# Turning rows of x and half results by VectorE blocks and a DRAM bounce instead of TensorE transposes, at the end of a decoder step

## The chip, the cores and the metric

The kernel runs on one core of one Trainium2 chip, in one launch. The metric is device time in microseconds (us) of that core, the median of several runs; lower is better. In the rows below PE is TensorE (PEld its weight loads), DVE is VectorE, ACT is ScalarE, POOL is GpSimd, and SP, SyncE, issues most of the DMAs. DMAs can also be issued from the ACT and POOL queues.

## The reference

One inference step of one decoder layer over 512 prompt rows and 8 x 4 sample rows, d_model 1024, all in float32. The part that the change touches is the end of the layer:

```python
    x = x + _rmsnorm(m, norm_mix_post[l])
    f, ffn_state = _conv_ffn(_rmsnorm(x, norm_ffn_pre[l]), ffn_prev, w_up[l], ffn_conv_w[l], ffn_conv_b[l], w_down[l])
    x = x + _rmsnorm(f, norm_ffn_post[l])

def _conv_ffn(h, prev, w_up, conv_w, conv_b, w_down):
    u = h @ w_up
    u, conv_state = _causal_dwconv(u, prev, conv_w, conv_b)
    val, gate = jnp.split(u, 2, axis=-1)
    return (jax.nn.gelu(gate, approximate=True) * val) @ w_down, conv_state
```

So each of the 544 token rows of `f` (1024 wide, summed over 4096 inner columns) is divided by its root mean square, multiplied by a gain, and added to `x`; the outputs are `y_p` (512 x 1024) and `y_s` (32 x 1024), token by token.

## The kernel before

Every float32 matrix is split into a high and a low part (`wh`/`wl`, `fH`/`fL`), and a product is three matmuls (high x high, high x low, low x high). Most of the kernel works transposed: feature on the partition, token on the free axis. The down projection's result is held in eight tiles `ft0` to `ft7`, tile c being features 128c to 128c+127 by 544 tokens. `HALF` cuts the tokens into half a=0 (tokens 0 to 255) and half a=1 (tokens 256 to 543: two prompt tiles and the 32 sample rows). The 4096 inner columns are eight groups q of four 128-blocks (`CH` = 4); `down(q, c, a, done)` adds group q to tile c, half a: 12 matmuls into a PSUM bank (`pmdn`), and then one VectorE addition into `ft` (`down_done`, or `last_done` for the last group).

The end of the kernel does the two halves differently.

- Half a=1 is finished transposed. For the last group (`QL`), a loop over c runs `down(QL, c, 1, last_done(c, acc))`. `last_done` adds the bank into `ft`, ScalarE squares the tile, and VectorE adds the square into `acc`; the square of tile 7 goes to `sq7`. `finish_b` then sums `acc` and `sq7` over the partitions with TensorE (`pst`), makes the reciprocal root (ScalarE and VectorE), scales the eight `ft` tiles on VectorE and adds x (`x1r`, read back from DRAM, feature by token) on GpSimd. `rows_t(2)`, `rows_t(3)`, `rows_t(4)` turn these tiles into token rows with TensorE transposes (`pyo`), ScalarE copies them to `yo`, and a DMA writes them.
- Half a=0 is finished token by token. Its last group is computed straight into token rows: `tokens(i, kk)` makes a 128 token x 512 feature bank (`ptok`) for token tile i and feature half kk, for (0,0), (0,1) and (1,0). The bank of (1,1) is cut in two banks of 256 features, `ends(0)` and `ends(1)` (`pend`), the last matmuls that a norm needs. The sum over the seven earlier groups sits in `ft` and is turned into token rows by TensorE: `turned(i, kk)` makes four transposes into `pfo`, and ScalarE copies them to `frow`; for (1,1) two float32 matmuls by the identity inside `ends` add it into the bank. `tokens_done` adds the bank to `frow` on VectorE, squares on ScalarE, multiplies by the gain `gpost` on GpSimd; `rstd`/`tokens_out` give the root and the output row, with x in token rows: `xtok[0, kk]`, turned by TensorE in `x1_rows` and copied by ScalarE, and for i=1 read from the PSUM bank `px`.

The order of the work: TensorE, ScalarE and VectorE run the end in the order in which the code records it. A `slot()` first runs what was left for this turn (`result(...)`, in front, and `later(k, f, ...)`, behind), so what `later` holds stands behind the additions of the bank that just ended. Three banks of group QL-1 (c = 5, 6, 7 of half a=0, the list `held`) are kept back and run after the loop, to cover the root of half a=1. SP's order is set by the scheduler in the loop and is written order after it.

Of the kernel before, what the change touches and what calls it, by code (L numbers as in the profile page):

```python
# [11 lines left out]
F32 = mybir.dt.float32  # L12
# [5 lines left out]
P = 128  # L18
# [49 lines left out]
DNS = 5  # L68
LAST_PLACES = {29: ('p3', 'p1', 'a22'), 30: ('p3', 'p1', 'a22'), 31: ('p1', 'a22')}
# [52 lines left out]
def hawk_step(ctx, tc, I, O):  # L122
# [1599 lines left out]
    def x1_rows(i, kk):  # L1722
        px = PX(f"px1{i}_{kk}")
        for j in range(4):
            pe.transpose(px[:, j * P:(j + 1) * P], x1r[4 * kk + j][:, i * P:(i + 1) * P], ident)
        return px

    def x1_again():
        for c in range(8):
            x1r[c] = S(f"x1r{c}")  # L1730
            nc.sync.dma_start(out=x1r[c][:, 0:NT], in_=x1d[c])
        yield 3
        for kk in range(2):
            px = x1_rows(0, kk)
            xtok[0, kk] = S(f"xtok0_{kk}")
            act.copy(xtok[0, kk][:, 0:512], px)
            yield 0.5
# [61 lines left out]
    def finish_b(acc):  # L1799
# [6 lines left out]
        for c in range(8):  # L1806
# [3 lines left out]
            if c % 2:  # L1810
                yield 0.5

    def rows_t(i, between=None):
# [3 lines left out]
        for kk in range(2):  # L1817
# [4 lines left out]
            if between and not kk:  # L1822
                between()
# [17 lines left out]
    def turned(i, kk):  # L1841
        px = PX(f"pfo{i}_{kk}")
        for j in range(4):
            pe.transpose(px[:, j * P:(j + 1) * P], ft[4 * kk + j][:, i * P:(i + 1) * P], ident)
        if i not in frow:
            frow[i] = RAW(f"frow{i}")
        later(1, act.copy, frow[i][:, kk * 512:(kk + 1) * 512], px)
# [15 lines left out]
    def tokens_done(i, kk, ps):  # L1863

        fr = frow[i][:, kk * 512:(kk + 1) * 512]
        add(fr, fr, ps)
# [3 lines left out]
        g = gpost[:, kk * 512:(kk + 1) * 512]  # L1870
# [11 lines left out]

    def ends(z):
        ps = PM(f"pend{z}")
        o = ps[:, 0:256]
        for k in range(CH):
# [3 lines left out]
            pe.matmul(o, fh, wh, start=k == 0, stop=False, skip_group_check=True)  # L1890
            if k == 0:
                for j in range(2):
                    pe.matmul(ps[:, j * P:(j + 1) * P], ft[4 + 2 * z + j][:, P:2 * P], ident, start=False, stop=False,
                              skip_group_check=True)
# [7 lines left out]
    def ends_gain(z, o):  # L1902
        mul(fgs[1, 1][:, 256 * z:256 * z + 256], o, gpost[:, 512 + 256 * z:768 + 256 * z])

    def tokens_out(i, r, z):
        x_ = xtok[i, z][:, 0:512]
        o = x_ if i == 0 else fgs[i, z]
# [90 lines left out]
```

## Time and profile before

| what | value |
|---|---|
| median of 3 runs | 974.34 us (974.23 to 974.61) |
| the profiled execution: its own time | 973.95 us |
| its span, first to last instruction | 972.2 us |
| TensorE clock granted over the span | 0.999 |
| busy share: PE, DVE, ACT, POOL | 99%, 78%, 57%, 17% |
| instructions: PE matmuls, DVE, ACT, POOL | 7634, 1599, 1349, 282 |

The profiled execution is 1.75 us longer than its span, and 0.39 us below the median. The span is what rows of the trace tell of; times in the rows are us from its start, and the end of the kernel is at 972.2 us. A row of the timeline gives the start, the duration (of all x instructions together), the engine, the line, the operation, the tiles written and read, and in brackets how long the engine stood idle before it and what ended that.

### The profile page before, as it was taken

The numbers are of one execution on the slowest core, as the hardware profiler recorded it, in microseconds if no ns is written. First come the engines' busy times: TensorE is split into PE (matmuls) and PEld (weight loads), VectorE is DVE, ScalarE is ACT, GpSimd is POOL, SyncE is SP. The second block draws the span as 40 slices with busy tenths as digits, with TensorE's granted clock in tenths as the row PEclk, the third lists the DMA queues.
The fourth block names the chain that finished last, engine by engine and source line by source line (L and its number), as shares of the span: only waits on it lengthen the run. The fifth ranks groups of instructions, "written<-read, shape, count | busy, mean of one in ns | idle before, by whom it ended". The sixth has DMA issues, their size and how long they took to land.

```text
span 972.2 us, 20023 instructions
## 1 busy us (share of the span) xinstructions
PE 963.0 (99%) x7634; PEld 955.2 (98%) x7634; DVE 756.3 (78%) x1599; ACT 553.9 (57%) x1349; POOL 167.9 (17%) x282
## 2 busy tenths in 40 slices
PE   9999999999999999999999999999999999999997
PEld 8999999999999999999999999999999999999996
DVE  5777888857858555599967888787888888888875
ACT  6544443467476425566767665655555555656653
POOL 2242000003406330230010111111011101020024
PEclk9999999999999999999999999999999999999999
DMA  7775535532334547135157575857576766668612
GB/s 229 236 213 180 151 89 147 162 93 87 108 110 128 179 115 189 52 121 186 45 117 182 128 198 123 192 130 181 136 181 157 171 155 156 170 145 219 201 31 92
DMA packets 234203, 143.07 MB, mean 147 GB/s; under 512 B 25012, under 2 KB 218940, under 8 KB 234076
## 3 DMA queue, kind: packets, MB, share of 16 engines
q1 hardware_dynamic: 224300, 120.21, 41.8%
q0 software_dynamic: 9696, 19.42, 11.8%
q10 hardware_dynamic: 112, 2.17, 0.6%
q8 instruction: 60, 0.98, 0.4%
q14 instruction: 35, 0.29, 0.1%
HBM read 115.59 MB, written 15.17 MB: 134 GB/s over the span
## 4 chain that ended last, share of the span: by engine, by line
PE 94%; DVE 3%; ACT 1%; issue 0%; DMA 0%; POOL 0%; SPq 0%; DVEq 0%; ACTq 0%; POOLq 0%
PE pmin L163 20%; PE pmdn L163 19%; PE pux L1527 16%; PE puy L1527 8%; PE pq L1527 6%; PE pmlo L163 5%; PE pmao L163 5%; PE pmout L163 4%; PE puz L1527 4%; PE pg L163 1%; PE pvp L163 1%; PE psc L163 1%; PE ptok L163 1%; DVE wl_e L166 0%; DMA pt<-pd 0%
## 5 line engine op out<-in xcount | busy, mean ns | idle before, releaser
L163 PE MATMUL pmin<-hH,wh_in 128*128 128x256 f32 (+1 forms) x568 | 164.0, 291 | 0.0
L163 PE MATMUL pmin<-hL,wh_in 128*128 128x256 f32 (+1 forms) x568 | 162.4, 288 | 0.0
L163 PE MATMUL pmin<-hH,wl_in 128*128 128x256 f32 (+1 forms) x568 | 159.1, 288 | 0.0
L163 PE MATMUL pmdn<-fH,wh_dn 128*128 128x256 f32 (+1 forms) x448 | 129.2, 288 | 0.0
L163 PE MATMUL pmdn<-fH,wl_dn 128*128 128x256 f32 (+1 forms) x448 | 129.0, 288 | 0.0
L163 PE MATMUL pmdn<-fL,wh_dn 128*128 128x256 f32 (+1 forms) x448 | 128.9, 288 | 0.0
L163 PEld LDWEIGHTS pmin<-hH,wh_in 128*128 128x128 f32 x568 | 107.2, 189 | 1.2 <-issue 1.0
L163 PEld LDWEIGHTS pmin<-hL,wh_in 128*128 128x128 f32 x568 | 107.2, 189 | 0.1
L163 PEld LDWEIGHTS pmin<-hH,wl_in 128*128 128x128 f32 x568 | 104.7, 188 | 0.2 <-issue 0.2
L175 DVE SCALAR_TENSOR_TENSOR uc<-u,fv,uc 128x560 f32<-128x560 f32 x128 | 102.0, 797 | 1.7 <-ACT uc L1558 1.1
L163 PEld LDWEIGHTS pmdn<-fH,wl_dn 128*128 128x128 f32 x448 | 84.4, 188 | 0.0
L163 PEld LDWEIGHTS pmdn<-fL,wh_dn 128*128 128x128 f32 x448 | 84.3, 188 | 0.1
L163 PEld LDWEIGHTS pmdn<-fH,wh_dn 128*128 128x128 f32 x448 | 84.2, 188 | 0.1
L1655 ACT COPY u<-pux 128x272 f32<-128x272 f32 x52 | 20.1, 387 | 86.0 <-PE pux L1527 86.0
L166 DVE TENSOR_TENSOR u<-puy,u 128x240 f32<-128x240 f32 (+2 forms) x78 | 24.6, 344 | 49.6 <-PE puy L1527 32.5
L172 DVE TENSOR_TENSOR ft<-ft,pmdn 128x256 f32<-128x256 f32 (+1 forms) x104 | 45.1, 434 | 16.7 <-PE pmdn L163 16.7
L281 ACT ACTIVATE wh_in<-raw_in 128x512 fp32r<-128x512 f32 x70 | 42.2, 625 | 19.0 <-issue 10.6
L288 DVE TENSOR_TENSOR wl_in<-raw_in,wh_in 128x512 fp32r<-128x512 f32 x70 | 47.8, 693 | 1.0 <-ACT wh_in L281 1.0
L1558 ACT ACTIVATE uc<-u,fv 128x560 f32<-128x560 f32 x64 | 48.2, 755 | 0.0
L779 ACT ACTIVATE s<-s,st 128x256 f32<-128x256 f32 (+1 forms) x32 | 15.2, 475 | 53.0 <-DVE st L776 42.5
L166 DVE TENSOR_TENSOR wl_dn<-raw_dn,wh_dn 128x512 fp32r<-128x512 f32 x56 | 38.3, 685 | 3.6 <-ACT wh_dn L1476 3.6
L1465 POOL DMA_DIRECT2D raw_up_s<-raw_up_s x26 | 22.4, 861 | 93.2 <-DMA raw_up_s<-raw_up__11237 5.5
(743 smaller groups left out, 3374.9 us busy)
## 6 DMA issues: line engine op xcount, KB each, us to landing
raw_in<-in_w_in_dram SPq DMA_DIRECT2D x35, 512.0 KB
raw_dn<-in_w_down_dram SPq DMA_DIRECT2D x56, 256.0 KB
raw_up_s<-in_w_up_dram SPq DMA_DIRECT2D x25, 512.0 KB
raw_up_s<-raw_up_s POOLq DMA_DIRECT2D x26, 256.0 KB, 4.3
raw_ao<-in_w_attn_o_dram SPq DMA_DIRECT2D x8, 512.0 KB
raw_lo<-in_w_lru_o_dram SPq DMA_DIRECT2D x8, 512.0 KB
raw_out<-in_w_out_dram SPq DMA_DIRECT2D x8, 512.0 KB
pd<-pb SPq DMA_DIRECT2D x12, 256.0 KB
```

What stands on the lines that cost most here:

```text
L163: pe.matmul(out, l, r, start=start, stop=stop)
L166: dve.tensor_tensor(out=out, in0=a, in1=b, op=ALU.subtract)
L172: dve.tensor_tensor(out=out, in0=a, in1=b, op=ALU.add)
L175: dve.scalar_tensor_tensor(out=out, in0=a, scalar=s_, in1=b, op0=op0, op1=op1)
L281: act.activation(hl[0], raw, AF.Copy)
L288: (eng or dve).tensor_tensor(out=hl[1], in0=raw, in1=f32(hl[0]), op=ALU.subtract)
L779: act.activation(s3[:, j, :], s3[:, j, :], AF.Exp, bias=ng[:, j:j + 1], accum_out=sm[:, j:j + 1])
L1465: pool.dma_start(out=w["p4"], in_=w["p2"], accum_op=ALU.add)
L1527: pe.matmul(ps[:, :HN], w, x, start=start and k == 0 and i == 0, stop=stop and k == 3 and i == 2, skip_group_check=True)
L1558: act.activation(yt[j][:, 0:FLATU], u[:, 0:FLATU], AF.Copy, scale=fv[:, j:j + 1])
L1655: act.copy(e[nm_], z)
```

## The change

It takes 40 matmuls out of TensorE's program: every `turned`, `x1_rows` and `rows_t(2)` transpose, and the identity matmuls of `ends`. In their place `blocks` turns 32 x 32 blocks on VectorE (`dve.transpose`), both token tiles of half a=0 in one instruction per 128-feature tile, or the third tile alone. `rows_of` writes the block-turned buffer to DRAM with one DMA and reads it back with four, each of which gathers one block row, so that the row tile holds tokens on its partitions; inside a partition the features stay in blocks of 32, which `by_block` undoes in the access pattern of the reader. Six such bounces stand in the program: `f0` (the half results of features 0 to 511, tokens 0 to 255), `x0` and `x1` (the same for x), `f1` (half results of features 512 to 1023, two of its reads from ACT's queue), and `y0`, `y1` (the finished third output tile). ScalarE puts the x rows in order (`x_natural`); GpSimd copies the third output tile in order (`yo2`). The banks of `ends` are begun by a ScalarE copy of the half results into PSUM (`ends_begin`), so that the matmuls go on from it. SP's DMAs keep written order from the start of the last loop. `gpost` becomes two half tiles.

```diff
+TURNS = {0: (("f", 0), ("f", 1)), 1: (("f", 2), ("f", 3)), 2: (("x", 0), ("x", 1)), 3: (("x", 2), ("x", 3)),
+         4: (("x", 4), ("x", 5)), 5: (("x", 6),), 6: (("x", 7),)}
...
-    def x1_rows(i, kk):
-        px = PX(f"px1{i}_{kk}")
-        for j in range(4):
-            pe.transpose(px[:, j * P:(j + 1) * P], x1r[4 * kk + j][:, i * P:(i + 1) * P], ident)
-        return px
...
+    def blocks(buf, j, src, n):
+        o = buf[:, 0:512 * n].rearrange("p (b i c d) -> p c i b d", i=n, b=4, c=4)[:, j]
+        dve.transpose(o, src.rearrange("p (i b q) -> p i b q", i=n, b=4))
+
+    def rows_of(buf, n, rows, nm, queues=(nc.sync,)):
+        w = 512 * n
+        dr = drp.tile([P, w], F32, name=f"{nm}_blocks")
+        nc.sync.dma_start(out=dr, in_=buf[:, 0:w])
+        src = dr.rearrange("(a q) (b x) -> b q a x", a=4, b=4)
+        for b in range(4):
+            queues[b % len(queues)].dma_start(out=rows[32 * b:32 * b + 32, 0:w].rearrange("q (a x) -> q a x", a=4),
+                                              in_=src[b])
+        r = rows[:, 0:w].rearrange("p (a i c d) -> p i c a d", a=4, i=n, c=4)
+        return [r[:, i] for i in range(n)]
+
+    def by_block(ap):
+        return ap.rearrange("p (c a d) -> p c a d", a=4, d=32)
...
             if c % 2:
                 yield 0.5
+                for z in (c - 3, c - 2) + ((6, 7) if c == 7 else ()):
+                    if z >= 0:
+                        y2_block(z)
...
+    def y2_block(c):
+        if c % 4 == 0:
+            ybuf[c // 4] = T(f"yb{c // 4}")
+        blocks(ybuf[c // 4], c % 4, ft[c][:, 2 * P:3 * P], 1)
+        if c % 4 == 3:
+            yrow[c // 4], = rows_of(ybuf[c // 4], 1, S(f"yrow{c // 4}"), f"y{c // 4}")
...
-    def turned(i, kk):
-        px = PX(f"pfo{i}_{kk}")
-        for j in range(4):
-            pe.transpose(px[:, j * P:(j + 1) * P], ft[4 * kk + j][:, i * P:(i + 1) * P], ident)
-        if i not in frow:
-            frow[i] = RAW(f"frow{i}")
-        later(1, act.copy, frow[i][:, kk * 512:(kk + 1) * 512], px)
...
-        fr = frow[i][:, kk * 512:(kk + 1) * 512]
-        add(fr, fr, ps)
+        fr = T(f"fr{i}_{kk}")[:, 0:512]
+        add(by_block(fr), frow[i, kk], by_block(ps[:, 0:512]))
...
+    def ends_begin(z):
+        pends[z] = PX(f"pend{z}")
+        act.copy(by_block(pends[z][:, 0:256]), frow[1, 1][:, 2 * z:2 * z + 2])
...
-            pe.matmul(o, fh, wh, start=k == 0, stop=False, skip_group_check=True)
-            if k == 0:
-                for j in range(2):
-                    pe.matmul(ps[:, j * P:(j + 1) * P], ft[4 + 2 * z + j][:, P:2 * P], ident, start=False, stop=False,
-                              skip_group_check=True)
+            pe.matmul(o, fh, wh, start=False, stop=False, skip_group_check=True)
...
+    def x_natural(i, z):
+        xnat[i, z] = S(f"xnat{i}_{z}")[:, 0:512]
+        act.copy(by_block(xnat[i, z]), xtok[i, z])
...
     def tokens_out(i, r, z):
-        x_ = xtok[i, z][:, 0:512]
-        o = x_ if i == 0 else fgs[i, z]
-        stt(o, fgs[i, z], r, x_, ALU.mult, ALU.add)
+        o = fgs[i, z]
+        stt(o, o, r, xnat[i, z], ALU.mult, ALU.add)
...
+    order_.enter_context(tc.manual_schedule(engines={nc.sync.engine}))
     for c in range(8):
         down(QL, c, 1, last_done(c, acc))
...
-        if c in (3, 5):
-            turned(c // 5, 0)
...
+        for what, z in TURNS.get(c, ()):
+            if what == "f":
+                later(1, block2, "f", ft, frow, z)
+                if z == 3:
+                    later(1, rows2, "f", frow, 0)
+            else:
+                later(1, block2, "x", x1r, xtok, z)
+                if z % 4 == 3:
+                    later(1, rows2, "x", xtok, z // 4)
...
     for _, q, c, a in held:
         down(q, c, a, down_done(q, c))
+        for z in range(4, 8) if c == HELD else ():
+            if z < HELD:
+                later(1, block2, "f", ft, frow, z)
+        later(1, block2, "f", ft, frow, c)
+        if c == 7:
+            later(1, rows2, "f", frow, 1, (nc.sync, act))
+            for i in range(2):
+                later(2, x_natural, i, 0)
         slot(0)
     for i, kk in ((0, 0), (0, 1), (1, 0)):
         ps = tokens(i, kk)
         if (i, kk) == (0, 0):
             slot(0)
-            turned(0, 1)
         slot(0)
+        if (i, kk) == (0, 1):
+            for z in range(2):
+                ends_begin(z)
         tokens_done(i, kk, ps)
+        if i == kk == 0:
+            for z in range(2):
+                x_natural(z, 1)
...
-    yo = [rows_t(2)]
+    yo2 = RAW("yo2")
+    for z in range(2):
+        pool.tensor_copy(by_block(yo2[:, 512 * z:512 * z + 512]), yrow[z])
+    yo = [lambda: nc.sync.dma_start(out=yp[2 * P:3 * P, :], in_=yo2)]
```

Three places of the program show how the order moves. The first is VectorE in the last loop: `ft`c is tile c of half a=1 taking its bank `pmdn_7_c_1`, and `acc31` takes the square that ScalarE made of it. Before:

```order
L172 TENSOR_TENSOR ft1_7004<-ft1_7004,pmdn_7_1_1_13223 128x288
L172 TENSOR_TENSOR acc31_13198<-acc31_13198,sq_ft1_1_13261 128x288
L172 TENSOR_TENSOR ft2_7154<-ft2_7154,pmdn_7_2_1_13247 128x288
L172 TENSOR_TENSOR acc31_13198<-acc31_13198,sq_ft1_2_13286 128x288
L172 TENSOR_TENSOR ft3_7258<-ft3_7258,pmdn_7_3_1_13266 128x288
L172 TENSOR_TENSOR acc31_13198<-acc31_13198,sq_ft1_3_13305 128x288
L172 TENSOR_TENSOR ft4_7386<-ft4_7386,pmdn_7_4_1_13291 128x288
```

After, with `fb0` the block buffer of the half results and `xb0` that of x:

```order
L174 TENSOR_TENSOR ft1_7004<-ft1_7004,pmdn_7_1_1_13218 128x288
L174 TENSOR_TENSOR acc31_13198<-acc31_13198,sq_ft1_1_13252 128x288
L1733 STREAM_TRANSPOSE fb0_13233<-ft2_7154 128x2x4x32
L1733 STREAM_TRANSPOSE fb0_13233<-ft3_7258 128x2x4x32
L174 TENSOR_TENSOR ft2_7154<-ft2_7154,pmdn_7_2_1_13238 128x288
L174 TENSOR_TENSOR acc31_13198<-acc31_13198,sq_ft1_2_13280 128x288
L1733 STREAM_TRANSPOSE xb0_13283<-x1r0_13057 128x2x4x32
L1733 STREAM_TRANSPOSE xb0_13283<-x1r1_13059 128x2x4x32
L174 TENSOR_TENSOR ft3_7258<-ft3_7258,pmdn_7_3_1_13266 128x288
L174 TENSOR_TENSOR acc31_13198<-acc31_13198,sq_ft1_3_13302 128x288
L1733 STREAM_TRANSPOSE xb0_13283<-x1r2_13061 128x2x4x32
L1733 STREAM_TRANSPOSE xb0_13283<-x1r3_13063 128x2x4x32
L174 TENSOR_TENSOR ft4_7386<-ft4_7386,pmdn_7_4_1_13288 128x288
```

Two block transposes now stand behind each addition of a square and ahead of the next addition of a bank.

The second is ScalarE behind the reciprocal root of half a=1 (`ry_o1`, `rw_o1`). Before, `pfo` was copied out between the squares `jk`:

```order
L1167 ACTIVATE ry_o1_13404<-pst_o1_13387,epst_95 128x288
L1168 ACTIVATE rw_o1_13405<-ry_o1_13404 128x288
L1868 ACTIVATE jk0_0_13460,ssq_13196<-frow0_13284 128x512
L1586 COPY frow0_13284<-pfo0_1_13450 128x512
L1868 ACTIVATE jk0_1_13479,ssq_13196<-frow0_13284 128x512
L418 ACTIVATE nst_t0_13484<-ssq_13196,epst_95 128x1
L1868 ACTIVATE jk1_0_13504,ssq_13196<-frow1_13330 128x512
```

After:

```order
L1169 ACTIVATE ry_o1_13419<-pst_o1_13399,epst_95 128x288
L1170 ACTIVATE rw_o1_13420<-ry_o1_13419 128x288
L1742 DMA frow1_13463<-f1_blocks_13464 32x4x256 x2
L1933 COPY xnat0_0_13477<-xrow0_13307 128x512
L1933 COPY xnat1_0_13479<-xrow0_13307 128x512
L1891 ACTIVATE jk0_0_13496,ssq_13196<-fr0_0_13494 128x512
L1933 COPY xnat0_1_13500<-xrow1_13377 128x512
L1933 COPY xnat1_1_13502<-xrow1_13377 128x512
L1910 COPY pend0_13529<-frow1_13463 128x256
L1910 COPY pend1_13531<-frow1_13463 128x256
L1891 ACTIVATE jk0_1_13535,ssq_13196<-fr0_1_13533 128x512
```

ScalarE now issues two of the reads of `f1`, which wait for the write to DRAM, and ahead of the square of `fr0_1` it has four row copies and the two copies that begin the banks `pend0` and `pend1` from `frow1`.

The third is SP's queue at the very end. Before:

```order
L1922 DMA gpost_13370<-in_norm_ffn_post_dram 128x1024
L1909 DMA out_0_dram<-xtok0_0_13219 128x512
L1909 DMA out_0_dram<-xtok0_1_13243 128x512
L1824 DMA out_0_dram<-yo2_13516 128x1024
L1824 DMA out_0_dram<-yo3_13569 128x1024
L1909 DMA out_0_dram<-fg1_0_13506 128x512
L1909 DMA out_0_dram<-fg1_1_13514 128x512
```

After, from the write of `f1` on:

```order
L1739 DMA f1_blocks_13464<-fb1_13416 128x1024
L1742 DMA frow1_13463<-f1_blocks_13464 32x4x256 x2
L1739 DMA y0_blocks_13484<-yb0_13470 128x512
L1742 DMA yrow0_13483<-y0_blocks_13484 32x4x128 x4
L1739 DMA y1_blocks_13523<-yb1_13517 128x512
L1742 DMA yrow1_13522<-y1_blocks_13523 32x4x128 x4
L1938 DMA out_0_dram<-fg0_0_13498 128x512
L1938 DMA out_0_dram<-fg0_1_13537 128x512
L1999 DMA out_0_dram<-yo2_13571 128x1024
L1845 DMA out_0_dram<-yo3_13608 128x1024
L1938 DMA out_0_dram<-fg1_0_13563 128x512
L1938 DMA out_0_dram<-fg1_1_13569 128x512
```

The outputs of token tile 0 (`fg0_0`, `fg0_1`) and all that follow now stand behind the writes and reads of `y0` and `y1`, each read behind its own write, and the last two outputs behind that of `yo2`.

38 lines of the change are left out of this document (21 added, 17 removed).

## The prediction

> **What bounds the kernel now.** I read the page first: the span, the busy shares and the chain that ended last.
>
> ```profile
> span 972.2 us, 20023 instructions
> PE 963.0 (99%) x7634; PEld 955.2 (98%) x7634; DVE 756.3 (78%) x1599; ACT 553.9 (57%) x1349; POOL 167.9 (17%) x282
> ...
> PE 94%; DVE 3%; ACT 1%; issue 0%; DMA 0%; POOL 0%; SPq 0%; DVEq 0%; ACTq 0%; POOLq 0%
> ```
>
> TensorE is busy for 99% of the span and carries 94% of the chain, so in most of the kernel a microsecond taken from its program is a microsecond gained. The change touches only the last 40 us, so the next view is the chain of waits there (start, duration, what).
>
> ```profile
> 932.20 0.44 PE px L1725 x4
> ...
> 937.86 0.44 PE pfo L1844 x4
> ...
> 946.51 0.97 PE pst_o L163 x4
> ...
> 953.09 0.44 PE pfo L1844 x4
> 953.52 5.58 PE ptok L163 x24
> 959.11 0.87 PE pyo L1820 x8
> ...
> 960.10 0.44 PE pend L1893 x4
> ...
> 963.58 0.12 PE pend L1896
> ```
>
> Up to 963.70 (963.58 + 0.12) the chain is one TensorE instruction behind the other, with no wait between them; the transposes are links of it. The other engines are hidden there, but only just, which the timelines of VectorE, ScalarE and TensorE show (in brackets the idle time before a row and who ended it).
>
> ```profile
> 933.23 0.44 DVE L1744 STREAM_TRANSPOSE ffn_rows_s<-sfT 128x256 f32<-128x256 f32 x1
> 933.59 0.42 DVE L172 TENSOR_TENSOR ft<-ft,pmdn 128x288 f32<-128x288 f32 x1
> ...
> 935.73 0.78 DVE L172 TENSOR_TENSOR ft<-ft,pmdn 128x288 f32<-128x288 f32 x2
> 937.48 0.46 DVE L172 TENSOR_TENSOR acc<-acc,sq_ft 128x288 f32<-128x288 f32 x1 [0.96 <-ACT sq_ft L1181]
> ...
> 938.82 0.46 DVE L172 TENSOR_TENSOR acc<-acc,sq_ft 128x288 f32<-128x288 f32 x1 [0.51 <-ACT sq_ft L1181]
> ...
> 942.46 0.46 DVE L172 TENSOR_TENSOR acc<-acc,sq_ft 128x288 f32<-128x288 f32 x1 [1.49 <-ACT sq_ft L1181]
> ...
> 945.50 0.45 DVE L172 TENSOR_TENSOR ft<-ft,pmdn 128x288 f32<-128x288 f32 x1
> ...
> 951.56 0.41 DVE L172 TENSOR_TENSOR ft<-ft,pmdn 128x256 f32<-128x256 f32 x1
> ```
>
> ```profile
> 940.02 0.57 ACT L1586 COPY frow<-pfo 128x512 f32<-128x512 f32 x1
> 940.60 1.28 ACT L1917 ACT_TABLE_LOAD   x1
> ...
> 945.98 0.45 ACT L1178 ACTIVATE sq<-ft 128x288 f32<-128x288 f32 x1 [0.89 <-DVE ft L172]
> ```
>
> ```profile
> 946.35 0.65 PE L163 MATMUL pst_o<-acc,ones 128*128 128x288 f32 x2
> 946.83 0.65 PE L163 MATMUL pst_o<-sq,ones 128*128 128x288 f32 x2
> ```
>
> VectorE adds the last bank of the last loop (945.50) only a moment before ScalarE squares it (945.98 to 946.43), and TensorE sums that square from 946.83 on. The slack between the square and its reader is 0.4 us. That is the narrowest place of the region, and the change puts VectorE work in front of it.
>
> **What goes from TensorE.** Ahead of the last bank stood two groups of `px` (four transposes each), three of `pfo`, and two of `pend` on line 1893, 0.44 us each, and the eight of `pyo` at 0.87: 7 x 0.44 + 0.87 = 3.95 us. Of that 4 x 0.44 = 1.76 stand ahead of the sum `pst_o`. The eight `px` behind the last bank and what follows them are not on the way to the last output row. If nothing else moved, the end would come 3.95 earlier, at about 970.4.
>
> **What comes to VectorE in the last loop.** Twelve block transposes of 256 columns stand between the addition of bank 0 and that of bank 7 (four of the half results, eight of x). The row of `ffn_rows_s` is the same operation on 128x256: 0.44 us, the next instruction 0.36 behind its start. Twelve make 12 x 0.36 = 4.3 us. Could they lie in the idle time of the additions to `acc` (0.51 each)? No: that idle time stands between the addition of a bank and the addition of its square, while the transposes stand behind the latter, ahead of the next bank. They lengthen the chain. What they do hide is ScalarE's extra delay: two waits were longer than 0.51, by 0.45 (937.48) and 0.98 (942.46), put there by the copies of `xtok` and `frow` and the table load in front of the squares. The copies go, and the table load now fits beside two transposes. So bank 7 is added at 945.50 + 4.3 - 1.4 = 948.4, its square is ready 0.93 later (945.50 to 946.43 before), at 949.3, and the second `pst_o` matmul begins there instead of at 946.83: 2.5 us late. TensorE would have been at the sum at 946.35 - 1.76 = 944.6 and idles some 4 us. The 1.76 is lost and 2.5 more is added to all that stands behind the root of half a=1.
>
> Both ends of the transposes' price: the row is the same operation at the same size, so I allow a seventh each way, 0.31 to 0.42, which is 0.6 to 0.7 us on the loop; what differs is that the new tile is written in runs of 32 elements. I take 0.36.
>
> **The second bounce of half results.** The bank that ends the first half's `ft7` was added at 951.56. Now it comes 2.5 later, and behind one block transpose more: 954.4. Then its own transpose, 0.8 with the addition ahead of it, and the buffer can leave at 955.0. The way through DRAM has a forerunner in this kernel, the attention's `pb` to `pd` to `pt` (write of 256 KB, then four reads), and its rows bound it.
>
> ```profile
> 114.17 0.34 SPq L824 DMA_DIRECT2D pd<-pb  x1
> 116.28 1.74 SPq L829 DMA_DIRECT2D pt<-pd  x4
> ...
> 143.57 0.34 SPq L824 DMA_DIRECT2D pd<-pb  x1
> ```
>
> ```profile
> 147.27 4.37 DMA pt<-pd
> ```
>
> ```profile
> DMA to landing us min/median/max: 2.0/3.8/6.5
> ```
>
> The quiet case: 2.1 us from the issue of the write to that of the first read (114.17 to 116.28), 0.43 for a second read on the same queue (1.74 / 4), and 2.0 to landing, the shortest of `ffn_rows_s`: 4.6 us. The loud case: 143.57 to 151.64 (147.27 + 4.37), 8.1 us, while weights were loading. No weights load at the end, so I stay near the quiet one, with twice the bytes in the write (512 KB; 256 KB more at the 401 GB/s quoted further down are 0.65): 5.3 us. `frow1` lands at 960.3. The Trainium skill, "DMA: Bandwidth & Descriptors", section "Anatomy of one DMA", gives about 2.0 us fixed and 436 KB per us; by it, as an estimate, the write takes 3.2 and a 128 KB read behind 0.43 of issue 2.7, 5.9 in all, and the sum below would be 0.6 higher. The earlier bounces (`f0`, `x0`, `x1`) end before their readers come: the last of them starts before the root, its readers come after it, and I cost them at nothing; SP has only the gain to issue beside them. Were that cover gone, the output rows of tile 0 would wait on `xnat`, at most for the rest of one bounce.
>
> Who waits for it? ScalarE's two copies that begin the banks of `ends`, and the addition for (0,1). TensorE, 2.5 late at the root, ends `ptok` at 959.1 + 2.5 - 0.44 = 961.2, so the two banks are begun in time or 0.3 late, and end near 964.5 (2 x 12 matmuls, 0.118 each, from 961.6) against 963.70: TensorE no longer sets the end.
>
> **VectorE's tail sets it.** Its rows before:
>
> ```profile
> 956.41 0.69 DVE L172 TENSOR_TENSOR frow<-frow,ptok 128x512 f32<-128x512 f32 x1 [2.15 <-PE ptok L163]
> ...
> 960.24 2.45 DVE L175 SCALAR_TENSOR_TENSOR xtok<-fg,nst_t,xtok 128x512 f32<-128x512 f32 x2
> 962.61 0.41 DVE L169 TENSOR_TENSOR fg<-pend,gpost 128x256 f32<-128x256 f32 x1
> ...
> 964.25 0.42 DVE L169 TENSOR_TENSOR fg<-pend,gpost 128x256 f32<-128x256 f32 x1 [0.79 <-ACT jke L1900]
> ...
> 965.39 1.41 DVE L175 SCALAR_TENSOR_TENSOR fg<-fg,nst_t,px 128x512 f32<-128x512 f32 x2
> ```
>
> ```profile
> 960.47 1.67 POOL L1874 TENSOR_TENSOR fg<-frow,gpost 128x512 f32<-128x512 f32 x1 [1.67 <-DVE frow L172]
> ```
>
> The addition for (0,1) was at 956.41, waiting for TensorE. It now waits for `frow1` until 960.4: 4.0 late. From there to the first multiplication of a bank is the root and two output rows, 6.2 us (962.61 - 956.41), whose ScalarE square now stands behind the bank copies: I give it nothing more, since the 2.15 us of the next bank's wait is gone as well. So 966.6. The rest to the last two rows is 2.78 less the 0.79 waited for the second bank, which is now long ready: 968.6. The last two rows took 1.41 with x in PSUM; the two before took 2.45 with all operands in SBUF while GpSimd multiplied (960.47). Now x comes from SBUF, and GpSimd copies `yo2` at that time: between 1.41 and 2.45 I take 1.8, as the cover by GpSimd is partial. VectorE ends at 970.4 against 966.80: 3.6 late.
>
> **SP's queue at the end.**
>
> ```profile
> 966.53 1.15 SPq L1909 DMA_DIRECT2D out_dram<-fg  x2
> ```
>
> ```profile
> 967.00:969.00 2.00, 0.00 (x0) 0.00 (x0) 0.00 (x0) 0.04 (x1) 0.00 (x0) 1.00 1.08 401
> ```
>
> The last output is issued 3.6 later. Its data also meets a longer queue: `yo2` (512 KB) went out ahead of these rows and now comes behind the bounce of `y1` and GpSimd's copies, so it leaves with the last 1 MB. At 401 GB/s that is 1.3 us if the DMA engines are full, nothing if not; I take 0.9.
>
> **The sum** is 3.6 + 0.9 = +4.5 us on the span: 976.7, and with the 1.75 us that the profiled execution has outside its span (973.95 - 972.2) 978.45. The median is 0.39 above that execution, so I predict 978.8 us.
>
> **The rivals.**
> - *VectorE keeps up* (the other side). If the transposes cost the chain nothing, the root comes 1.76 early, the buffer leaves at 951.56 - 1.76 + 0.4 = 950.2, `frow1` lands at 954.8 with the quiet bounce, and the tail starts 1.6 earlier and is 0.79 shorter: 974.34 - 2.4 = 971.9. This decides near a price of zero for each transpose; at 0.15 us (12 x 0.15 - 1.43 = 0.4, the slack) the root is just where it was, and the bounce still costs. The bracketed waits speak for spare time, the order of the instructions against its use. 4%.
> - *Short tail, about no change.* The bounce takes 4.6, the last rows 1.41, the outputs do not queue: 978.8 - 0.7 - 0.4 - 0.9 = 976.8, and at 0.31 us a transpose 976.2. 12%.
> - *A loud bounce.* 8.1 us, because six bounces and their reads meet on the same DMA engines: 978.8 + 2.8 = 981.6. Against it: no weight loads there. 13%.
> - *TensorE's clock falls in its new idle time.*
>
> ```profile
> 966.00:968.00 2.00, 0.33 (x3) 0.04 (x1) 0.80 (x2) 1.03 (x3) 0.00 (x0) 1.00 0.55 227
> ...
> 970.00:971.00 1.00, 0.00 (x0) 0.00 (x0) 0.00 (x0) 0.00 (x0) 0.00 (x0) 0.87 0.35 133
> 971.00:972.00 1.00, 0.00 (x0) 0.00 (x0) 0.00 (x0) 0.00 (x0) 0.00 (x0) 0.50 0.00 0
> ```
>
> After the last matmul (0.33 us busy from 966.0) the granted clock stays whole for over 3.7 us and is half by 971. TensorE's new pause is about 4 us. If it trips, some 3 us of matmuls take twice as long, the two banks end at about 967.5 instead of 964.5, and VectorE waits about 1 us for the second: 979.8. 9%. The Trainium skill, "TensorE: Matmul & The Clock Gate", section "What's actually happening", has a free-running window of about 3.4 us of idleness after which the clock is halved; by that rule this rival would be likely, by the rows it is at the edge.
>
> **How the numbers follow.** The forecast has 62%. The range 975.5 to 982.0 leaves out the first rival, the shortest tails and the loudest bounces, some 15%. A measurement of this kernel tells 0.2% (1.95 us) from no change: faster is below 972.4, slower above 976.3. Faster 0.04 (the first rival), the same 0.12 (the second), slower 0.84.
>
> **What would show it.** In the profile of the changed kernel: an idle time of TensorE of 3 to 5 us ahead of `pst_o`; block transposes of about 0.44 us, and bank 7 added near 948.4; `fr0_1` at about 960.4, waiting for a DMA on `frow1`; the chain of waits at the end through VectorE and DMA instead of TensorE; the last rows slower than 0.7 us each beside GpSimd. I am wrong if TensorE's rows still run without a gap into the sum, or if `frow1` lands before 957.

## The result, and the profile after

The changed kernel takes 985.12 us (median of 4 runs, 984.20 to 985.35) against 974.34 for the kernel before: a ratio of 1.0108, 95% interval 1.0093 to 1.0123, or 10.8 us lost. I had said 978.8 us, 975.5 to 982.0: the direction is right, the size is not. The profiled execution took 985.35 with a span of 983.6, 11.4 more than the span before.

The page, at the same places as before:

```profile
span 983.6 us, 20023 instructions
PE 963.4 (98%) x7590; PEld 954.3 (97%) x7590; DVE 763.4 (78%) x1623; ACT 553.7 (56%) x1348; POOL 169.8 (17%) x284
...
PE 88%; DVE 6%; DMA 2%; ACT 2%; issue 1%; SPq 0%; DVEq 0%; POOL 0%; ACTq 0%; POOLq 0%
```

44 matmul rows are gone (the 40 matmuls taken out; each of the four by the identity in `ends` shows as two rows), yet TensorE's share of the chain fell from 94 to 88%: the end now runs through VectorE, ScalarE and DMA. TensorE's timeline has two gaps where it had none (in brackets the idle time and who ended it):

```profile
948.24 1.22 PE L165 MATMUL pst_o<-acc,ones 128*128 128x288 f32 x2 [3.12 <-DVE acc L174]
949.40 1.33 PE L165 MATMUL pst_o<-sq,ones 128*128 128x288 f32 x2
967.25 0.58 PE L1918 MATMUL pend<-wh_dl,fH 128*128 128x256 f32 x1 [4.81 <-ACT pend L1910]
```

VectorE's timeline from the last bank on:

```profile
948.46 0.75 DVE L174 TENSOR_TENSOR ft<-ft,pmdn 128x288 f32<-128x288 f32 x2
...
951.78 0.46 DVE L177 SCALAR_TENSOR_TENSOR rw_o<-pst_o,rw_o 128x288 f32<-128x288 f32 x1 [1.90 <-ACT rw_o L1170]
...
955.71 0.45 DVE L1733 STREAM_TRANSPOSE fb<-ft 128x256 f32<-128x256 f32 x1
...
966.85 0.69 DVE L174 TENSOR_TENSOR fr<-frow,ptok 128x512 f32<-128x512 f32 x1 [6.32 <-DMA frow<-f_blocks]
...
974.65 1.76 DVE L177 SCALAR_TENSOR_TENSOR fg<-fg,nst_t,xnat 128x512 f32<-128x512 f32 x2
```

The row at 966.85 is the addition for (0,1). It stood at 956.41 before: 10.44 of the 11.4 us are there already. What it waited for stands in the timeline of SP, the queue that issues the bounces (start, time of the issues on the queue, how many), and in the chain of waits, which has the DMAs' own time from issue to landing:

```profile
944.78 0.38 SPq L1739 DMA_DIRECT2D x_blocks<-xb  x1
948.25 1.74 SPq L1742 DMA_DIRECT2D xrow<-x_blocks  x4
950.09 0.85 SPq L1952 DMA_DIRECT2D gpost<-in_norm_ffn_post_dram  x2
951.04 0.38 SPq L1739 DMA_DIRECT2D x_blocks<-xb  x1
956.96 1.75 SPq L1742 DMA_DIRECT2D xrow<-x_blocks  x4
958.80 0.38 SPq L1739 DMA_DIRECT2D f_blocks<-fb  x1
...
976.80 2.37 SPq L1938 DMA_DIRECT2D out_dram<-fg  x2
```

```profile
944.78 3.43 DMA x_blocks<-xb
...
951.04 5.85 DMA x_blocks<-xb
...
958.80 3.61 DMA f_blocks<-fb
962.43 0.39 ACTq L1742
962.85 3.87 DMA frow<-f_blocks
```

`f1`'s last block is turned at 956.16 (955.71 + 0.45), but its write leaves at 958.80. SP works in order, and ahead of it stand the reads of `x1`, which wait for `x1`'s write (5.85 us, against 3.43 for the same write of `x0`), which stood behind the reads of `x0` and the two broadcasts of the gain. From its write to the addition `f1` then takes 8.05 us (958.80 to 966.85). ScalarE, which issues two of the reads, stood 11.66 us up to 963.41 on the same write, but it caught up: it waited 0.62 us more for `frow` before it copied the banks.

So I set out three theories. A: SP's order and the traffic of the bounces hold `f1`. B: the twelve block turns in the last loop, which delay the root and stop TensorE. C: TensorE's clock after the two gaps. A fourth, D, came with the end of the trace: the third tile's two bounces crowd the last 10 us.

### The profile page after: what moved, and what is told of

The parts are those of the page before. It is cut to its first block, busy times and chain, and to the rows that moved or that the text cites. A ratio compares the mean times of both kernels' runs of the same rounds, so it can differ in the third digit from the quotient of the medians.

```text
span 983.6 us, 20023 instructions
## 1 busy us (share of the span) xinstructions
PE 963.4 (98%) x7590; PEld 954.3 (97%) x7590; DVE 763.4 (78%) x1623; ACT 553.7 (56%) x1348; POOL 169.8 (17%) x284
## 4 chain that ended last, share of the span: by engine, by line
PE 88%; DVE 6%; DMA 2%; ACT 2%; issue 1%; SPq 0%; DVEq 0%; POOL 0%; ACTq 0%; POOLq 0%
PE pmin L165 20%; PE pux L1529 16%; PE pmdn L165 16%; PE puy L1529 8%; PE pq L1529 6%; PE pmlo L165 5%; PE pmao L165 5%; PE pmout L165 4%; PE puz L1529 4%; PE pg L165 1%; DMA x_blocks<-xb 1%; PE pvp L165 1%; PE psc L165 1%; DVE wl_e L168 0%; DVE wl_dl L168 0%
```

## The experiments

In each kernel the row to look at is the addition for (0,1); its start and the time of the kernel go together, with one exception. The start is from the profiled execution, the time is the median. Line numbers shift by a few from kernel to kernel, and starts by 0.1 to 0.2 us already ahead of the region (one row stands at 922.16 in the changed kernel and at 921.97 with the clock kept). The diffs are shortened, with the switches of the kernels resolved, and the remarks behind `#` tell what else moves.

| kernel | addition (0,1) | median us | ratio to before, 95% |
|---|---|---|---|
| before | 956.41 | 974.3 | |
| changed | 966.85 | 985.12 | 1.0093 to 1.0123 |
| turns alone (before + 12 turns) | 959.52 | 976.96 | 1.0019 to 1.0040 |
| f on TensorE | 959.32 | 976.48 | 1.0015 to 1.0033 |
| x on TensorE | 960.42 | 977.98 | 1.0023 to 1.0053 |
| third tile on TensorE | 966.54 | 982.45 | 1.0068 to 1.0098 |
| gain early | 962.99 | 981.55 | 1.0058 to 1.0092 |
| f1 on ScalarE's queue | 964.37 | 981.42 | 1.0057 to 1.0088 |
| clock kept | 968.02 | 986.19 | 1.0107 to 1.0137 |
| x late | 961.77 | 985.29 | 1.0098 to 1.0128 |
| turns in the wait | 965.43 | 983.90 | 1.0083 to 1.0113 |
| all mended | 961.63 | 977.26 | 1.0018 to 1.0042 |
| x and third tile, in the wait | 956.45 | 973.51 | 0.9982 to 1.0001 |
| x alone, in the wait | 956.61 | 974.07 | 0.9988 to 1.0007 |

### One part undone

**f back on TensorE.**

```diff
-                later(1, block2, "f", ft, frow, z)        # and the bounces f0, f1
+            turned(c // 5, 0)                             # four transposes, a copy by ScalarE
```

> Edit: only the rows of the half result f go back to TensorE (16 transposes against the identity, the copies by ScalarE, and the identity matmuls in the last banks); the rows of x and the third output tile keep their block turns and their DRAM bounces. Theory A (the loss is the bounce of f1: its write stands on SP's queue behind x1's bounce, and the bounce takes 8.0 us): without that bounce nothing of the tail waits for a DMA of f, so some 8 us of the 10.8 go and the time is about 976 to 978. Theory B (the loss is the block turns on VectorE in the last loop, which make the root late and stop TensorE): 8 of the 12 turns are still there, so at most a third of the loss goes: about 982.

Measured: 976.48 us (the profiled execution 975.71), 8.6 less than the changed kernel, as A says. The addition still comes 2.9 late (959.32 against 956.41), though nothing of f goes through DRAM. ScalarE's timeline says why:

```profile
957.66 1.14 ACT L1976 COPY xnat<-xrow 128x512 f32<-128x512 f32 x2 [0.71 <-DMA xrow<-x_blocks]
958.71 0.58 ACT L1589 COPY frow<-pfo 128x512 f32<-128x512 f32 x1
```

The copy of `frow` stands in ScalarE's order behind two copies of x that wait for `x1`'s bounce. The bounce that I had costed at nothing is what a reader waits for here as well.

**x back on TensorE.**

```diff
-                later(1, block2, "x", x1r, xtok, z)       # and the bounces x0, x1
+        px = x1_rows(0, kk); act.copy(xtok[0, kk][:, 0:512], px)
```

> Edit: only the rows of x go back to TensorE (16 transposes); f and the third output tile keep their block turns and bounces. Theory A (SP's queue stands in order on x1's write, and x1's reads share the DMA engines with f1): f1's write leaves when its last block is turned, near 955 instead of 958.8, its bounce takes 5 to 6 us instead of 8.0, and some 6 us of the loss go: 977 to 979. Theory B (turns in the loop): 8 of 12 turns are gone, the root comes some 2 us earlier and nothing else changes: about 983. Theory C (the clock after TensorE's pauses): the pause ahead of the root's sums is shorter, the one ahead of the last banks also; no more than 2 us of its own.

This kernel leaves out a part of the last rows: as far as its code tells, what ScalarE lays into the last two banks does not reach the output, and no run settles why. Every instruction is still run, so its time is read. Measured: 977.98, 7.1 less, in A's range. With nothing of x on SP the write of `f1` leaves when its last block is turned, and the chain of waits has the price of that bounce alone:

```profile
953.27 2.61 DMA f_blocks<-fb
955.91 0.39 ACTq L1757
956.34 3.87 DMA frow<-f_blocks
960.42 0.70 DVE fr L175
```

From the write to the addition 7.15 us: the write is shorter by 1.0 than in the changed kernel, the reads are not. The addition comes 6.4 earlier, and not all of it is A's: 2.9 because the last block is turned earlier (953.25 against 956.16, with eight turns less in the loop), 2.6 because its write no longer waits for the queue, 0.9 because the bounce is shorter.

**The third tile back on TensorE.**

```diff
-        pool.tensor_copy(by_block(yo2[:, 512 * z:512 * z + 512]), yrow[z])   # and the bounces y0, y1
+    yo = [rows_t(2)]
```

> Edit: only the third output tile goes back to TensorE (8 transposes and two copies by ScalarE); x and f keep their block turns and bounces. Theory A: y0's write is issued behind f1's reads and so delays f1 only through the shared DMA engines: a gain of 0 to 1.5 us, 983.5 to 985. Theory D (the crowded end: the two bounces of the third tile, GpSimd's copies beside VectorE's last rows, the tile's own output among the last issues, are what costs): the last issue on SP ends some 3 us earlier, 981 to 982.

Measured: 982.45, 2.7 less, between the two ranges and nearer to D's. The addition moved by only 0.31 (966.54), so y0 does not delay `f1`: D, not A. VectorE's last two rows and SP's last issue:

```profile
974.32 1.41 DVE L178 SCALAR_TENSOR_TENSOR fg<-fg,nst_t,xnat 128x512 f32<-128x512 f32 x2
```

```profile
975.10 1.13 SPq L1981 DMA_DIRECT2D out_dram<-fg  x2
```

1.41 instead of 1.76 for the rows without GpSimd's copies beside them, and the last two issues begin 1.7 earlier and take 1.13 instead of 2.37: they end at 976.23 instead of 979.17.

### The turns by themselves, and moved

**Twelve turns that nobody reads, in the kernel before.**

```diff
+        for what, z in TURNS.get(c, ()):
+            later(1, spare_turn, what, z)        # dve.transpose of the same block into an unread tile
```

> The kernel before, with the same twelve block turns on VectorE put in the last loop at the same places, written to buffers that nothing reads: no DMA, nothing taken from TensorE. Theory B alone is measured: the last bank's addition comes some 3 us later (the turns are 0.36 to 0.44 us each, 12 of them 4 to 5 us, and VectorE has 1 to 2 us of slack in that loop), and all of it reaches the end: about 977.5 (976.5 to 978.5). Theory A says that the turns alone cost little of the 10.8 us, so under 979 in any case; if it comes to 981 or more, the turns are the larger part and A falls.

Measured: 976.96, 2.7 us over the kernel before (974.28 in the runs beside it), in the range that B gave. The second sum of the root begins at 949.84 (946.83 before), and no clock falls: the pause ahead of the first is short.

```profile
948.67 0.75 PE L165 MATMUL pst_o<-acc,ones 128*128 128x288 f32 x2 [1.60 <-DVE acc L174]
949.84 0.75 PE L165 MATMUL pst_o<-sq,ones 128*128 128x288 f32 x2 [0.41 <-ACT sq L1180]
```

**The turns in the wait for a square**, the changed kernel otherwise.

```diff
             act.activation(sq[:, :n], src, AF.Square)
+            for f in between:                    # the turns, here instead of behind the addition
+                f()
             add(acc[:, :n], acc[:, :n], sq[:, :n])
```

> The changed kernel with one thing moved: each block turn of the last loop stands between the addition of a bank and the addition of its square, where VectorE waits 0.51 us for ScalarE's square, instead of behind both. Nothing is added or taken away. Theory B in its narrow form (the turns cost because they stand outside that wait; 0.35 us each of 12 would be 4.2, and 2.7 were measured for them alone): one turn in a bank fits into the wait, two take 0.70 and overrun it by some 0.2, so the root comes 2 to 2.5 us earlier than in the changed kernel, TensorE's pause ahead of it falls from 3.1 to about 1 us, and x's and f1's bounces move with it: 982 to 983. Theory A alone (SP's queue sets the end whatever the root does): x1's write stands behind x0's reads and the two broadcasts, which move only in part: 984 to 985.

Measured: 983.90, 1.2 less, between the two ranges. The root is back where it was before the change (`rw_o` at 948.49, 3.3 earlier; 948.53 before), more than I expected, and yet only 1.2 of it arrives. SP again:

```profile
950.24 0.38 SPq L1758 DMA_DIRECT2D x_blocks<-xb  x1
955.82 1.75 SPq L1761 DMA_DIRECT2D xrow<-x_blocks  x4
957.67 0.38 SPq L1758 DMA_DIRECT2D f_blocks<-fb  x1
```

`f1`'s last block is turned at 952.87 (952.42 + 0.45 in VectorE's timeline), and its write now waits 4.8 us for the queue instead of 2.6. That is A: a root 3.3 earlier lets the write go only 1.1 earlier (957.67 against 958.80), and the rest lengthens the wait on SP. The turns cost 2.7 alone, but with SP in front of `f1` most of that is hidden behind the queue.

### The queue

**The gain's broadcasts early.**

```diff
-        if c == 6:
+        if c == 0:
             for z in range(2):
                 gpost.append(S(f"gpost{z}")[:, 0:512])
```

> The changed kernel with the two broadcasts of the gain vector issued at the first bank of the last loop instead of the seventh; nothing else. They now stand on SP's queue ahead of x1's write (2 x 0.43 us), and x1's write takes 5.85 us behind them where x0's took 3.43 without. Theory A (the loss is SP's queue and what shares the DMA engines): x1's write leaves 1 us earlier and takes some 3.5 us, so f1's write leaves when its last block is turned, at 956.2 instead of 958.8; its bounce still takes 7 to 8 us: 982 to 983. Theory B (turns) and theory C (clock): no change, 985.

Measured: 981.55, 3.6 less, a little past the range that A gave:

```profile
949.70 0.38 SPq L1754 DMA_DIRECT2D x_blocks<-xb  x1
953.16 1.74 SPq L1757 DMA_DIRECT2D xrow<-x_blocks  x4
956.03 0.34 SPq L1754 DMA_DIRECT2D f_blocks<-fb  x1
```

The write of `x1` is followed by its reads 3.46 us later instead of 5.92, and `f1` leaves at 956.03, when its last block is turned. The two broadcasts, 0.85 us of issue, held the queue for 0.95 us (950.09 to 951.04 in the changed kernel), and `x1`'s write, which runs beside the 2 x 256 KB that they put into SBUF, took 2.5 more.

**f1's bounce on ScalarE's queue.**

```diff
-        nc.sync.dma_start(out=dr, in_=buf[:, 0:w])
+        queues[0].dma_start(out=dr, in_=buf[:, 0:w])
...
-            later(1, rows2, "f", frow, 1, (nc.sync, act))
+            later(1, rows2, "f", frow, 1, (act,))
```

> The changed kernel with f1's bounce (its write and all four reads) issued from ScalarE's queue, where nothing of x stands ahead of it. Theory A in its narrow form (the order on SP's queue is what holds f1): the write leaves at 956.2 instead of 958.8 and the row addition comes 2.6 us earlier: 982.5. Theory A in its wide form (the 16 DMA engines are shared, and f1 would only collide with x1's write and reads): the bounce becomes longer by as much as it starts earlier, 984.5 to 985. Theories B and C: 985. A rival of its own: ScalarE itself waits for f1's turns before it can issue, and its squares behind that come late; then 985 or more.

Measured: 981.42, 3.7 less, more than either form of A gave. The write leaves at 955.67, ScalarE's timeline:

```profile
955.67 0.36 ACTq L1754 DMA_DIRECT2D f_blocks<-fb  x1
958.47 2.25 ACTq L1757 DMA_DIRECT2D frow<-f_blocks  x4
```

The way through DRAM became longer, 8.7 us (955.67 to 964.37) against 8.05, so the addition gains 2.5 of the 3.1. It is not the write: the reads begin 2.80 after it, against 3.63 (958.80 to 962.43). The four reads now stand on one queue and take 2.25 us to issue, against 0.86 for two on each of two queues, and in the chain of waits the last of them follows the landing of a read of `x1`:

```profile
957.16 3.23 DMA xrow<-x_blocks
960.41 3.79 DMA frow<-f_blocks
```

So the order on SP is what was taken away, which is A in its narrow form; how much of the longer way is the single queue and how much the sharing with `x1`'s reads isn't separated. The rest of the gain is at the end, where the last rows take 1.41 again and the last two issues 1.40 instead of 2.37.

**x's bounces behind f1.**

```diff
-                later(1, block2, "x", x1r, xtok, z)      # in the last loop
+            if c in (5, 7):                              # behind the held banks 5 and 7
+                for z in range(4): later(1, block2, "x", x1r, xtok, 4 * (c // 7) + z)
```

> All parts of the change stay, only their order differs: the block turns of x and its two bounces go behind the held banks 5 and 7, behind f1's write on SP's queue. Four turns instead of twelve stay in the last loop. Theory A: f1's write leaves when its last block is turned and meets only x's traffic behind it, its bounce takes some 7 us as in the kernel with the rows of x on TensorE, and the loss falls by some 6 us; x1's rows then come at about 968 to 970 and may be what the last rows wait for: 979 to 982. Theory B: the eight turns moved out of the loop are worth some 2 us and the rest stays: 983.

Measured: 985.29, no gain; neither theory had that. The addition for (0,1) did come 5.1 earlier (961.77). What ate it is ScalarE's timeline:

```profile
966.75 1.14 ACT L1976 COPY xnat<-xrow 128x512 f32<-128x512 f32 x2 [7.04 <-DMA xrow<-x_blocks]
967.80 0.67 ACT L1948 COPY pend<-frow 128x256 f32<-128x256 f32 x2
968.41 0.62 ACT L1929 ACTIVATE jk<-fr 128x512 f32<-128x512 f32 x1
```

ScalarE has to copy `x1`'s rows ahead of the two banks and of the square of the row just added, and stood 7.04 us on the bounce that had been put last. The wait changed its engine, not its length.

### The clock

```diff
+        keep_warm(12)        # ahead of pst_o: mm(pk[:, ...], ones, ones, True, True), read by nobody
...
+    keep_warm(20)            # ahead of the last banks
```

> The changed kernel with matmuls that nothing reads in TensorE's two pauses: 12 ahead of the sums of the root and 20 ahead of the last banks. They take away the low clock (0.83 in the stretch of the root, 0.50 in that of the last banks) and nothing else. Theory C (the clock after the pauses is a large part): the root comes 0.8 us earlier, the last banks end 2.3 us earlier, 982 to 983. Theory A (TensorE is not what the end waits for): only the 0.8 us of the root can reach the end, and f1's write is held by SP's queue anyway: 984.3 to 985.

Measured: 986.19, 1.1 more, above the ranges of both theories. The root came 0.8 earlier (`rw_o` at 951.00; 0.2 of it is there ahead of the region already) and its sums were at full clock, 0.75 instead of 1.22 and 1.33. SP issued `f1`'s write at 958.70, as in the changed kernel (958.80), so nothing of it arrived: at the root C is out. At the second gap the clock was not kept, it fell 1.3 us after the last banks had begun; there it is the chain of waits that speaks against C, which in the changed kernel has no piece of TensorE from 929.82 to its end. The reads of `f1` took 5.16 us instead of 3.87; what made them slower isn't settled, and it is the 1.1 that was lost.

### The mends together

**All parts of the change, three mends**: the turns in the wait, the gain early, `f1` on ScalarE's queue.

> All parts of the change, with the three mends together: the turns in the wait of each bank, the gain's broadcasts at the first bank, f1's whole bounce on ScalarE's queue. If the causes add up (turns 2.0 to 2.5 us by the kernel before, SP's queue 3.6 us by the early gain), what is left is f1's own way through DRAM (6.9 us from write to landing where nothing of x is in flight) and the crowded end: 978.5 to 979.5. If the early gain and ScalarE's queue take away different waits, up to 2 us less: 977. If something else holds the end, 980.5 or more.

Measured: 977.26, 7.9 of the 10.8 us back. That is the number I had put at 977, but not for the reason I gave. The early gain and ScalarE's queue (3.6 and 3.7 alone) take away the same wait, that of `f1`'s write behind SP: each lets it go when its last block is turned, and both together can't do more. What adds to it is the earlier root, which no queue hides any longer: the block is turned at 953.15 instead of 956.16 and its write leaves at 953.18 instead of 958.80, the bounce takes 0.4 more, and the addition comes 5.2 earlier; the profiled execution gains another 2.4 behind it. The kernel is still 3.0 over the kernel before, with the addition at 961.63: TensorE made those rows by 956.41, and the way through DRAM, 8.45 us here (953.18 to 961.63), cannot be hidden, since its source is ready no earlier.

```profile
953.18 3.54 DMA f_blocks<-fb
...
958.11 3.35 DMA frow<-f_blocks
```

**Only what can be hidden**: x and the third tile, f on TensorE.

```diff
+TURNS = {0: (("x", 0), ("x", 1)), 1: (("x", 2),), 2: (("x", 3),), 3: (("x", 4),), 4: (("x", 5),), ...
-        if c == 6:                               # the gain's broadcasts
+        if c == 0:
-                later(2, x_natural, i, 0)
+                for z in range(2): later(2, x_natural, i, z)
```

> A version that may beat both: f goes back to TensorE (no bounce on the path to the end), x and the third tile stay on VectorE; x's eight turns stand in the waits of seven banks, the gain's broadcasts at the first bank, and ScalarE's four copies of x behind the root, ahead of the squares. By the reasons so far (a bounce costs nothing where it lands well before its reader, a turn nothing inside the wait for a square): TensorE has 24 transposes less, 16 of them ahead of the last bank's end at 0.11 us each, 1.75 us, of which some 1 to 1.5 reach the end: 972.8 to 973.6. If VectorE's tail or the third tile's bounce at the end decides: 974 to 976, as f on TensorE alone (976.5).

Measured: 973.51 against 974.24 in the runs beside it, ratio 0.9992, interval 0.9982 to 1.0001: inside the forecast 972.8 to 973.6, but only 0.7 us. Its ten runs all lie under those of the kernel before (973.08 to 973.82, against 974.06 to 974.60), yet the interval still holds no change. The turns fit into the wait: ahead of the additions to `acc` 0.16 us of idleness are left of 0.51, and `pst_o` waits 0.21.

```profile
943.34 0.44 DVE L1749 STREAM_TRANSPOSE xb<-x1r 128x256 f32<-128x256 f32 x1
943.93 0.46 DVE L174 TENSOR_TENSOR acc<-acc,sq_ft 128x288 f32<-128x288 f32 x1 [0.16 <-ACT sq_ft L1185]
```

**x alone, in the wait**: the same with the third tile on TensorE.

> As the last one, but the third tile is on TensorE as well: of the change only the rows of x are left, turned in the waits of the banks. TensorE has 16 transposes less, 8 of them ahead of the last bank's end (0.87 us). By the reasons so far: 973.4 to 974.2; the difference to the kernel with the third tile turned too says what the third tile's bounce costs or brings at the end. If it is 975 or more, the turns of x cost something that the wait doesn't hide.

Measured: 974.07, ratio 0.9998 (0.9988 to 1.0007): no change, inside its range. Turning x on VectorE costs nothing when its turns stand in the wait and its bounce ends early, and it brings nothing either. The third tile's bounce, which cost 2.7 at the changed kernel's crowded end, brings 0.6 here: the ten runs of the two kernels don't overlap (this one has 973.90 to 974.56), but it is less than the 0.9 us that each interval has to either side.

## Why the prediction was wrong, and where it was right

Right: bank 7 is added at 948.46 (I wrote 948.4), TensorE's gap ahead of `pst_o` is 3.12 us (3 to 5), the second `pst_o` begins at 949.40 (949.3), the chain at the end goes through VectorE and DMA, and the last rows are slow beside GpSimd, 1.76 us (1.8). The turns alone, measured in the kernel before, cost 2.7 us where I had put 2.5 at the root.

Wrong is one row, the addition for (0,1): 960.4 in the prediction, 966.85 in the trace, 6.45 us late, and the time was missed by 6.3. Three terms make it up in the trace.

- *"The earlier bounces end before their readers come ... I cost them at nothing; SP has only the gain to issue beside them."* This is the step that failed, with 2.64 us (956.16 to 958.80). I looked at who reads a bounce and not at what stands behind it on its queue: the reads of `x1` wait there for their write, and `f1`'s write waits behind them. That the gain's broadcasts would slow that write I had not costed. The early gain and ScalarE's queue show both.
- *"I stay near the quiet one ... 5.3 us."* From its write to the landing the bounce took 7.92 (958.80 to 962.85 + 3.87): 2.62 more, the length of the loud rival (8.1, 13%). 1.9 of it is the reads, 0.9 the write. I had taken 2.0 us for a read from another DMA, the shortest of `ffn_rows_s`, though the forerunner's own read, 4.37, stood among my rows; the reads took 3.87 here and with nothing of x in flight too. The write took 3.61 with `x1`'s reads beside it, 2.61 without. The kernel with x on TensorE is the quiet case: 6.94 us from write to landing (953.27 to 956.34 + 3.87), well above both my value and the estimate of 5.9 from the fit of the Trainium skill ("DMA: Bandwidth & Descriptors", section "Anatomy of one DMA — SWDGE (gpsimd) path"), which is stated there for DMAs that GpSimd issues, while these came from SP and ScalarE. By the fit of the Trainium skill, as an estimate, the write takes 3.2, between the two measured, and a 128 KB read 2.3; the trace has 3.87, so for these reads the measurement decides.
- *"the buffer can leave at 955.0"*: 956.16, 1.2 late. The terms of the prediction themselves add up to 955.2 (954.4 and 0.8). About 0.6 is the clock: from the start of the second sum to ScalarE's root it is 1.37 us (949.40 to 950.77), and 0.79 with the clock kept. This term did not decide by itself: with the clock kept the block is turned 0.8 earlier, and the write leaves at 958.70 all the same.

The clock, which I gave 9%, did fall, in both gaps. It didn't matter, but not for the reason I gave it: not because the gap is short, but because the queue hid it at the root, and VectorE's rows at the end.

The end: from the addition to the end of the span I had 16.3 us (960.4 to 976.7), and 16.75 were measured. The third tile on TensorE makes it 14.2 (966.54 to 980.7), so its bounces cost 2.6 at the end, and I had put them at 0.9 and a part of the slow rows.

What the change could have brought was small in any case: with the bound undone everywhere that I found, 24 transposes less on TensorE gave 0.7 us of the 1.75 that their groups ahead of the last bank had taken (two of `px`, one of `pyo`): the root came no earlier than before (`rw_o` at 948.41 against 948.53).

## What to carry to other kernels

A detour through DRAM costs more than its own latency: all that stands behind its reads on the issuing queue waits for its write too, so ask of each bounce what is issued after it, and put the urgent one on a queue of its own. Engine work moved into a loop is free only at the place in the order where that engine waits; twelve turns cost 2.7 us behind the addition and nothing that could be seen at the root inside the wait for the square. Where a tail hangs on one row, follow that row's start from kernel to kernel: here the span less that start lies between 14.2 and 16.8 us in 13 of the 14 profiled executions, and the one with 22.2 (x late) sends to another wait.

## What the runs showed of the hardware

A 512 KB write to DRAM took 2.61 us with nothing beside it (x on TensorE) and 3.4 to 3.6 beside the reads of another bounce in most kernels, but 4.74 with x late, where `x1`'s write ran beside the reads of `f1` on two queues. Behind two broadcasts of a 512-element row to 128 partitions, whose issues took 0.85, it took 5.85.

TensorE's clock was half at the first matmuls after the gap of 3.12 us in the changed kernel, whole after a gap of 1.77 us in the kernel with x on TensorE. The windows of the changed kernel at the second gap (span, then PE, weight loads, VectorE, ScalarE, GpSimd, granted clock, DMA share, GB/s), where TensorE stopped at 962.44:

```profile
964.00:965.00 1.00, 0.00 (x0) 0.00 (x0) 0.00 (x0) 1.00 (x4) 0.00 (x0) 1.00 1.00 305
965.00:966.00 1.00, 0.00 (x0) 0.00 (x0) 0.00 (x0) 1.00 (x4) 0.00 (x0) 0.73 1.09 293
966.00:967.00 1.00, 0.00 (x0) 0.00 (x0) 0.15 (x1) 0.38 (x2) 0.00 (x0) 0.50 0.30 111
```

It fell some 3.0 us after the last matmul; in the kernel before it was still whole 3.7 us after its last. With the third tile on TensorE the first sum behind the same gap of 3.12 us still ran at full clock (0.75), and only the second did not (1.32). In the kernel with the clock kept it fell even so, after a gap of 2.81 us and in the middle of the last banks:

```profile
968.00:969.00 1.00, 0.58 (x4) 0.58 (x5) 0.69 (x1) 0.94 (x3) 0.21 (x1) 1.00 0.00 0
969.00:970.00 1.00, 1.00 (x10) 1.00 (x9) 0.50 (x1) 0.46 (x2) 1.00 (x1) 0.87 0.15 47
970.00:971.00 1.00, 1.00 (x7) 1.00 (x6) 0.72 (x6) 0.29 (x1) 0.07 (x1) 0.50 0.43 126
```

These changes keep to a beat of 3.41 us, not to a distance from the last matmul. In windows of 0.1 us the changed kernel's clock falls at 948.39 and 965.46 and rises at 951.81 and 972.29: 5, 1 and 7 times 3.41 us from the first. The kernels with the third tile on TensorE, the early gain, the clock kept, x late and the turns in the wait show the same step, each from another start. In the 3.41 us ahead of a fall TensorE was busy for 0.29 and 0.39 us in the changed kernel, 1.33 with the clock kept and 1.47 with x late, while the clock stayed whole over such a stretch with 1.73 (x on TensorE, up to 960.70) and 2.01 (`f1` on ScalarE's queue, up to 966.70). So whether a pause of some 3 us cost the clock depended on where the beat fell.

The Trainium skill, "TensorE: Matmul & The Clock Gate", section "What's actually happening", has a window of about 3.4 us that runs freely, and the half clock after at least one idle window. The trace agrees on the length and on the free run; that the window must be idle throughout it does not bear out, with 1.33 and 1.47 us of work in two of them.
